# Seven products of halves in place of the down projection of both MLPs, in an fp32 two-layer streaming trunk

## The chip, the cores and the metric

The kernel runs on one core of one Trainium2 chip. The metric is the device time of one execution in microseconds; a timed comparison takes the median of several executions. The core has five engines that work through queues of their own: TensorE (PE, with its weight loads listed apart as PEld), VectorE (DVE), ScalarE (ACT), GpSimd (POOL) and SyncE (SP), which issues loads. Each engine takes its queue in order, and waits on semaphores that other engines and DMAs raise.

## The reference

One inference step over 1152 tokens (1024 of a new stream, 8 x 16 of running streams) through two layers of width 1024. What matters here is the MLP at the end of each layer and the next norm:

```python
def sq_relu_mlp(h, w_up, w_down):                 # w_up (1024, 4096), w_down (4096, 1024)
    return jnp.square(jax.nn.relu(h @ w_up)) @ w_down

xp = xp + op                                      # mixer's output
xp = xp + sq_relu_mlp(rmsnorm(xp, norm_ffn[layer]), w_up[layer], w_down[layer])
y_prompt = rmsnorm(xp, norm_final)                # after both layers
```

All data is fp32. The kernel keeps fp32 accuracy by splitting each operand into a rounded part and a remainder (`hi`, `lo`, type fp32r) and adding three matmuls for each product: hi*hi, hi*lo, lo*hi (`SPLIT`).

## The kernel before, in words

Activations lie with features on partitions and tokens along a row. `mixer0` and `mixer1` are the attention and convolution stages of the two layers. `rest(layer, ...)` does what follows each mixer: the output projection, then the up projection, then the down projection. The MLP's inner layer has 32 blocks of 128 rows (`NF`).

**Up projection.** `unit(m)`, m = 0 to 15, makes two of these blocks, 2m and 2m+1. It already works by seven products of halves: the input's feature halves and token halves (`combo`), and the weights' halves with their sums, made by `seven`. A product k is `mms(k, n, ...)`: 4 chunks of 128 features x 3 parts = 12 matmuls of 288 columns for each n (0 and 1, a quarter of the tokens each), so 24 for a product and 168 for a unit. `take(k, n)` adds the results from PSUM on DVE (L1400 to L1412). `done` multiplies a quarter by the norm's factor (DVE, L1386), applies relu and square (ACT, L1387 and L1388), and stores a token half of a block from the POOL queue (L1390) to a buffer in HBM, `hid_d`. The hidden rows lie in four tiles (`hids`: `th` and three called `hdm`), two for even units and two for odd ones.

**Down projection.** It loads the hidden blocks back whole (`down_h`, L1469, 128 x 1152), splits them, loads the weights in pieces of 128 x 512 (`down_w` through `staging`, L187), splits them, and takes four inner blocks at a time (`NB`): for each of 8 output chunks c and 3 token groups g of 384 (`G`), `down(j, c, g)` issues 4 x 3 = 12 matmuls of 384 columns (L1485) into a PSUM bank, and DVE adds the bank to the residual `x[c]` in SBUF (L1489). That is 8 x 8 x 3 x 12 = 2304 matmuls for a layer. On the last four blocks the code also prepares the next stage: norm statistics and split inputs for layer 1's mixer (`Then0`), or the final norm, transposes and stores (`Then1`).

`split(hi, lo, src)` is a copy on ACT (L180) and a subtraction on DVE (L181). PSUM has 8 banks, handed out in a ring by `bank`; a bank is taken again once its last reader is through. Tiles of a pool with one name are handed on in the same way.

**What sets the order.** The program is written out as a list of operations; a scheduler then sets the order on each engine by its own estimate of when operands and tiles come free. So weight loads and splits are moved up as soon as their tile is free, and stand in an engine's queue ahead of work that was written before them.

## Time and profile before

| | us |
|---|---|
| three timed runs | 2881.17, 2886.65, 2888.04 (median 2886.65) |
| profiled execution: its time / its span | 2879.29 / 2877.5 |
| PE busy in the span | 2778.7 (97%) |
| DVE / ACT / POOL busy | 2015.6 / 1264.4 / 282.3 |
| up projection, layer 0 / layer 1 | 644.6 to 1009.2 / 2093.7 to 2460.0 |
| down projection, layer 0 / layer 1 | 1009.2 to 1413.6 / 2460.0 to 2865.4 |

Times inside the span count from its start. Where two durations overlap (a matmul starts before the one ahead of it has drained), rates are read from start to start over many instructions, not from the mean duration. "Idle before" is the time an engine sat still ahead of a group, with what ended it. KB are 1024 bytes.

### The profile page before, as it was taken

The page shows a single profiled execution, that of the slowest core. Times are in us where ns is not written, and L with a number is a line of the kernel's source. Part 1 is how long each engine was busy: PE and PEld are TensorE (multiplying, and loading weights), DVE is VectorE, ACT ScalarE, POOL GpSimd, SP SyncE. Part 2 cuts the span into 40 slices and gives each one's busy share as a digit, 9 for nine tenths or more (in the row PEclk, how much of TensorE's full clock was granted, in tenths as well). Part 3 has the DMA queues.
Part 4 walks back from the last instruction along what each step waited for, and adds up shares of the span by engine and source line. Part 5 has one row for each costly group of instructions (what it writes and reads, how often), then busy time and mean ns, then how long its engine had stood idle before and what let it go on. Part 6 is the DMA issues. An engine that isn't in the chain of part 4 may idle for free.

```text
span 2877.5 us, 48092 instructions
## 1 busy us (share of the span) xinstructions
PE 2778.7 (97%) x18586; PEld 2674.3 (93%) x18586; DVE 2015.6 (70%) x3939; ACT 1264.4 (44%) x2644; POOL 282.3 (10%) x511
## 2 busy tenths in 40 slices
PE   8988988899999999999999999998999999999998
PEld 8987876799999999999999999997999999999998
DVE  8999999988666654444567777778786666644445
ACT  5344446665555531211355555556555554411112
POOL 1000101031000000000111111110310110000001
PEclk9999998999999999999999999999999999999999
DMA  4434346443332362321344444446532322732311
GB/s 152 131 102 127 114 123 205 147 162 117 106 105 94 131 232 77 109 79 46 107 141 133 135 143 139 134 132 220 180 123 94 102 99 102 251 102 67 110 34 66
DMA packets 136004, 357.70 MB, mean 124 GB/s; under 512 B 21232, under 2 KB 44976, under 8 KB 133728
## 3 DMA queue, kind: packets, MB, share of 16 engines
q1 hardware_dynamic: 105936, 252.06, 27.5%
q0 software_dynamic: 29696, 102.56, 10.5%
q8 instruction: 146, 2.39, 0.3%
q14 instruction: 82, 0.67, 0.1%
q10 hardware_dynamic: 144, 0.02, 0.0%
HBM read 252.90 MB, written 89.03 MB: 119 GB/s over the span
## 4 chain that ended last, share of the span: by engine, by line
PE 75%; DVE 16%; ACT 4%; issue 3%; DMA 2%; POOL 0%; DVEq 0%; SPq 0%; ACTq 0%; POOLq 0%
PE pd L1485 28%; PE um L1380 23%; PE psc L220 10%; DVE y L671 4%; DVE kp L847 2%; PE avc L404 2%; PE psoa L220 2%; PE tpc L392 2%; PE f L220 1%; DVE sg L849 1%; PE zc L1137 1%; DVE wla L181 1%; PE zc L1138 1%; PE psp L220 1%; PE zs L505 1%
## 5 line engine op out<-in xcount | busy, mean ns | idle before, releaser
L1489 DVE TENSOR_TENSOR sl<-sl,pd 128x384 f32<-128x384 f32 x384 | 211.6, 552 | 342.4 <-PE pd L1485 342.0
L220 PE MATMUL psc<-h,hl_wc 128*128 128x384 f32 x1728 | 328.2, 340 | 0.0
L220 PEld LDWEIGHTS psc<-h,hl_wc 128*128 128x128 f32 x1728 | 298.5, 189 | 13.4 <-issue 11.5
L1380 PE MATMUL um<-sl,hl_m 128*128 128x288 f32 x1548 | 240.3, 296 | 0.0
L1380 PEld LDWEIGHTS um<-sl,hl_m 128*128 128x128 f32 x1548 | 217.7, 188 | 0.0
L671 DVE SCALAR_TENSOR_TENSOR y<-u,dw,y 128x1024 f32<-128x1024 f32 (+1 forms) x232 | 176.4, 807 | 0.4
L220 PE MATMUL psp<-h,hl_wi 128*128 128x384 f32 x864 | 169.7, 345 | 0.2 <-ACT kps L896 0.2
L220 PEld LDWEIGHTS psp<-h,hl_wi 128*128 128x128 f32 x864 | 150.4, 191 | 6.4 <-issue 4.9
L1485 PE MATMUL pd<-hsm,wdm 128*128 128x384 f32 x864 | 150.8, 334 | 0.0
L1485 PEld LDWEIGHTS pd<-hsm,wdm 128*128 128x128 f32 x864 | 149.9, 188 | 0.0
L181 DVE TENSOR_TENSOR hl_m<-xr,hl_m 128x512 fp32r<-128x512 f32 x132 | 92.4, 700 | 57.1 <-ACT hl_m L180 55.8
L180 ACT ACTIVATE hl_m<-xr 128x512 fp32r<-128x512 f32 x132 | 82.2, 623 | 104.7 <-PE um L1380 83.2
L1387 ACT ACTIVATE hdm<-hdm 128x288 f32<-128x288 f32 x192 | 84.8, 442 | 91.7 <-DVE hdm L1386 90.9
L1380 PE MATMUL um<-sl,hl 128*128 128x288 f32 x756 | 119.4, 296 | 0.0
L1104 ACT ACTIVATE s<-s,mxc 128x640 f32<-128x640 f32 (+4 forms) x128 | 88.8, 694 | 59.8 <-DVE mxc L1101 58.1
L1380 PEld LDWEIGHTS um<-sl,hl 128*128 128x128 f32 x756 | 106.6, 188 | 0.8
L180 ACT ACTIVATE wdm<-st_wd 128x512 fp32r<-128x512 f32 x40 | 23.8, 624 | 171.2 <-PE pd L1485 144.8
L1101 DVE CUSTOM_DVE_ANT_0 s<-zc,bp 128x384 f32<-128x384 f32 (+3 forms) x128 | 66.0, 517 | 38.9 <-PE zc L1138 38.1
L180 ACT ACTIVATE whc<-tpc 128x512 fp32r<-128x512 f32 (+1 forms) x144 | 72.5, 523 | 47.0 <-PE tpc L392 46.1
L181 DVE TENSOR_TENSOR wlc<-tpc,whc 128x512 fp32r<-128x512 f32 (+1 forms) x144 | 83.5, 595 | 12.8 <-ACT whc L180 10.4
L1390 POOL DMA_DIRECT2D hid_d<-hdm x96 | 51.9, 540 | 412.9 <-ACT hdm L1388 334.7
L180 ACT ACTIVATE hl<-st_wd 128x512 fp32r<-128x512 f32 x20 | 12.6, 629 | 171.0 <-PE pd L1485 155.3
(495 smaller groups left out, 6997.6 us busy)
## 6 DMA issues: line engine op xcount, KB each, us to landing
hrm<-hid_d SPq DMA_DIRECT2D x64, 576.0 KB, 5.0
xr<-in_w_up_dram SPq DMA_DIRECT2D x64, 512.0 KB, 3.7
st_wd<-in_w_down_dram SPq DMA_DIRECT2D x128, 256.0 KB, 3.3
hid_d<-hdm POOLq DMA_DIRECT2D x96, 288.0 KB, 2.4
st_wc<-in_w_in_c_dram SPq DMA_DIRECT2D x48, 256.0 KB, 2.7
xm_d<-xo POOLq DMA_DIRECT2D x16, 576.0 KB, 3.5
xr<-xm_d SPq DMA_DIRECT2D x16, 576.0 KB, 4.6
xr_d<-xr POOLq DMA_DIRECT2D x16, 576.0 KB, 3.3
```

The source lines that it names most:

```text
L180: ACT(hi, src, AF.Copy)
L181: return tt(lo, src, f(hi), ALU.subtract)
L220: mm(ps()[:, :G], hl[:, a, at:at + P], act[g][k // 4][b][:, k % 4, :], start=n == 0, stop=n == len(todo) - 1)
L392: nc.tensor.transpose(tp[:, c0 + q * P:c0 + (q + 1) * P], blocks.get(j, tile_q), ident)
L404: mm(st["av"][:, o0:o0 + n], vs[:, j, i].rearrange("p a d -> p (a d)"), src[:, c0:c0 + n], start=st["done"] == 0, stop=st["done"] == nmm - 1)
L671: stt(src if j == CW - 1 else dst, src, wj, dst, ALU.mult, ALU.add)
L1101: nc.vector.tensor_tensor_reduce(s[:, c:c + m], z, b, -1.0, mx, ALU.add, ALU.min, new)
L1104: ACT(s[:, :n], s[:, :n], AF.Exp, bias=mx, scale=-1.0, accum_out=tot)
L1380: mm(banks[b, n][:, :TQ], w[:, a, c * P:c * P + P], combo(key, c)[:, h, n * TQ:n * TQ + TQ], start=k < 3 and c == 0 and i == 0, stop=c == ...
L1387: ACT(y, y, AF.Relu)
L1485: mm(ps[:, :G], w[:, a, c % 4 * P:c % 4 * P + P], hid[NB * j + e][b][:, g * G:g * G + G], start=n == 0, stop=n == 3 * NB - 1)
L1489: tt(xs, xs, ps[:, :G], ALU.add)
```

## The change

The down projection becomes seven products too. The 32 inner blocks are paired (2j, 2j+1, j = 0 to 15), the outputs are halved (512 features each) and the tokens are halved (576 each, `TW`). With a11, a12, a21, a22 for the weights of a pair (first index: output half, second: inner block) and b11, b12, b21, b22 for the hidden rows (first: inner block, second: token half), the hidden operands are b11 (product 0), t2 = b11 - t3 (1), b12 - b11 (2), b21 (3), t3 = b12 - b22 (4), b22 (5) and t4 = b21 - t2 (6). A product runs over all 16 pairs before the next one starts, in PSUM, so that an output tile is added to the residual only where a product ends.

- The up projection now stores the seven operands, 128 x 576 each, to `hb_d`. Four subtractions on DVE are added to a unit: t3, t2 and b12 - b11 in `done` (after.py's L1400 to L1402), and t4 in `last_sum` (L1365), which is called in the next unit, before its product 2.
- The down projection is a list of 112 items (`todos`): 7 products x 16 pairs. An item loads its hidden operand (L1506), splits it (128 x 576) and the weight (128 x 512), and issues 4 output chunks x 2 token quarters x 3 = 24 matmuls of 288 columns (L1577). The products run in four chains that each hold all 8 PSUM banks: (3), (0, 1, 4), (2, 5), (6). Loads are written four items ahead, splits two.
- Weights a11, a21 and a22 are loaded once and stay in SBUF (`resident`, L1493), in tiles that the up projection leaves. Sums of weights are made on DVE (L1527 to L1533). a12 and, for the last product, a22 are loaded by item.
- What follows each layer now starts from finished quarters of the result (`then0`, `then1`). At the start of layer 1's mixer the token groups are taken in the order 2, 0, 1. In layer 1 the last product is done for one token quarter and then the other; the transposed part of the output shrinks from 384 to 288 tokens.
- The statistics tiles change with it: one tile `t1` (128 x 1152) is a buffer for squares, and holds t3 and t2 during the up projection.

The diff, cut to its core:

```diff
-    hid_d = [dram.tile([NF, P, T], F32, name=f"hid_d{l}") for l in range(2)]
+    hb_d = [dram.tile([7, NF // 2, P, TW], F32, name=f"hb_d{l}") for l in range(2)]
...
-                if p == 0 and (n, g) in ((1, 0), (0, 1)):
-                    (nx.end if n else nx.run_rows)(NG - 1)
-                if g == 0:
+                if p == 0 and n < 2:
+                    if n == 0:
+                        nx.run_rows(g)
+                    elif g == 2:
+                        nx.end(0)
+                        nx.end(1)
...
-                    return (chunks_steps([0, 1], got, ahead, h, ks, lambda n, ps, g: staged(0, n, ps, g), "c")
+                    return (chunks_steps([0, 1], got, ahead, h, ks, lambda n, ps, g: staged(0, n, ps, g), "c", gs=(2, 0, 1))
...
+        extra = own("t1", F32)
...
+        t3, t2 = extra[:, :TW], extra[:, TW:]
+        def last_sum(m):
+            t4 = hids[m % 2 * 2 + 1][:, :TW]
+            tt(t4, t4, t2, ALU.subtract)
+            put(hb_d[layer][6, m], t4)
...
-                    put(hid_d[layer][2 * m + e, :, half * TW:half * TW + TW], hd[e][:, half * TW:half * TW + TW])
+                    b11, b12, b22 = hd[0][:, :TW], hd[0][:, TW:], hd[1][:, TW:]
+                    if (e, half) == (0, 1):
+                        tt(t3, b12, b22, ALU.subtract)
+                        tt(t2, b11, t3, ALU.subtract)
+                        tt(b12, b12, b11, ALU.subtract)
+                        for k, t in ((4, t3), (1, t2), (2, b12)):
+                            put(hb_d[layer][k, m], t)
+                    else:
+                        put(hb_d[layer][{(0, 0): 0, (1, 1): 5, (1, 0): 3}[e, half], m],
+                            hd[e][:, half * TW:half * TW + TW])
...
             for k in range(start, 7):
                 seven(7 * m + k + 2)
+                if m and k == 2:
+                    last_sum(m - 1)
+                if m == NF // 2 - 1 and k > 4:
+                    begin(k - 5)
...
+        chains = ((3,), (0, 1, 4), (2, 5), (6,))
+        out = {3: [(0, 0)], 0: [(0, 0)], 1: [(0, 1)], 4: [(1, 0), (1, 1)], 2: [(1, 1)], 5: [(0, 1)], 6: [(1, 0)]}
+        final = {0: (0, 0), 2: (1, 1), 5: (0, 1), 6: (1, 0)}
+        todos = [(k, (0, 1), j) for chain in chains for k in chain for j in range(NF // 2)]
+        if layer == 1:
+            todos[6 * 16:] = [(6, (n,), j) for n in range(2) for j in range(NF // 2)]
+        wd = ins["w_down"][layer]
...
+        def resident(kind, j):
+            to = {"a11": a11, "a21": a21, "a22": a22}[kind]
+            if j % 2 == 0:
+                if kind == "a22":
+                    tag = ("sl8", "sl9", "sl10", "sl11", "lo0", "lo1", "lo2", "xr3")[j // 2]
+                    t = own(tag, F32)
+                else:
+                    t = place(j // 2, 0 if kind == "a11" else 1, F32, f"w{name}")
+                to[j], to[j + 1] = halves_of(t)
+            row = 2 * j + (kind == "a22")
+            dma(to[j], wd[row][:, :512] if kind == "a11" else wd[row][:, 512:])
+        def load(i):
+            if i >= len(todos):
                 return
+            k, ns, j = todos[i]
+            if i == 0:
+                for n in range(2):
+                    t = own(f"xr{n}", F32)
+                    braw.extend([t[:, :TW], t[:, TW:]])
+            cols = slice(ns[0] * TQ, ns[-1] * TQ + TQ)
+            bs[i] = braw[i % 4][:, :cols.stop - cols.start]
+            dma(bs[i], hb_d[layer][k, j][:, cols])
+            if k in (3, 5) or k == 6 and ns[0] == 0:
+                streams[i] = staging(wd[2 * j + 1][:, 512:] if k == 6 else wd[2 * j + 1][:, :512], f"wd{layer}{i}")
...
+        def split_w(i):
...
+            if k == 3 or k == 6:
+                src = streams.pop(i)
+            elif k == 5:
+                src = streams.pop(i)
+                tt(src, src, a22[j], ALU.subtract)
+            elif k == 1:
+                tt(a21[j], a21[j], a11[j], ALU.subtract)
+                tt(a22[j], a22[j], a21[j], ALU.add)
+                src = a22[j]
+            elif k == 2:
+                tt(a11[j], a11[j], a22[j], ALU.add)
+                src = a11[j]
+            else:
+                src = a11[j] if k == 0 else a21[j]
+            if k == 6 and layer == 1:
+                w = pair(place(j // 2, j % 2, F32R, f"wk{name}"))
+            elif k == 6:
+                if j < 8:
+                    tag = ("sl8", "sl9", "sl10", "sl11", "lo0", "lo1", "lo2", "xr3")[j]
+                    asplit.append(pair(own(tag, F32R)))
+                w = asplit[j % 8]
+            elif i % 6 < 4:
+                w = sp.tile([P, 2, 512], F32R, "hl", f"hl_wd{layer}{i}")
+            else:
+                w = pair(few[i % 6 - 4])
+            split(w[:, 0], w[:, 1], src)
+            ws[i] = w
+        def begin(n):
+            if n == 0:
+                for i in range(4):
+                    load(i)
+            else:
+                prep(0)
+                prep(1)
...
+        def item(i):
+            k, ns, j = todos[i]
+            first = any(k == chain[0] for chain in chains) and j == 0
+            b, w = bs.pop(i), ws[i]
+            for m in range(4):
+                for n in ns:
+                    if first:
+                        banks[m, n] = bank(f"pd{layer}{k}{m}{n}")
+                    ps = banks[m, n][:, :TQ]
+                    for s, (a, h) in enumerate(SPLIT):
+                        mm(ps, w[:, a, m * P:m * P + P], b[:, h, (n - ns[0]) * TQ:(n - ns[0]) * TQ + TQ],
+                           start=first and s == 0, stop=j == NF // 2 - 1 and s == 2,
+                           skip_group_check=not any(k == chain[0] for chain in chains))
+                    if j == NF // 2 - 1:
+                        for e, half in out[k]:
+                            xs = x[4 * e + m][:, half * TW + n * TQ:half * TW + n * TQ + TQ]
+                            tt(xs, xs, ps, ALU.add)
+            if j == NF // 2 - 1 and k in final:
+                later.extend(then(x, *final[k], None if len(ns) > 1 else ns[0], sq))
...
+        sq = Turns([extra[:, :TW], extra[:, TW:]])
+        for i in range(len(todos)):
+            if i == 3:
+                last_sum(NF // 2 - 1)
+            if 2 <= i < 18:
+                resident("a11", i - 2)
+            if 14 <= i < 30:
+                resident("a21", i - 14)
+            if 16 <= i < 32:
+                resident("a22", i - 16)
+            c = {n: m for m, n in enumerate((6, 7, 8, 9, 40, 41, 42, 43))}.get(i)
+            if c is not None:
+                x[c] = own(f"sl{c}", F32)
+                dma(x[c], xr_d[layer][c])
+            load(i + 4)
+            prep(i + 2)
+            item(i)
+            if i == 104 and soon:
+                soon()
+            for _ in range(1 + (len(later) > len(todos) - i)):
                 if later:
                     later.pop(0)()
...
+        def then0(x, e, half, n, sq):
+            n1.sq = sq
+            cols = slice(half * TW, half * TW + TW)
+            cs = range(4 * e, 4 * e + 4)
+            def square(c):
+                n1.square(x[c][:, cols], c, cols, c == (4 if half else 0))
+                put(x_d[:, c, cols], x[c][:, cols])
+            squares = [lambda c=c: square(c) for c in cs]
+            splits = [lambda c=c: n1.split(x[c][:, cols], c, cols) for c in cs]
+            if (e, half) == (0, 0):
+                early.extend(splits)
+                return squares
+            if (e, half) == (1, 1):
+                return squares + splits + early
+            if (e, half) == (0, 1):
+                return squares + splits
+            return [lambda: n1.end(2)] + [go for two in zip(splits, squares) for go in two]
```

How this moves instructions, at three places. First, DVE in an up projection's unit, around the additions of its last product (k = 6). `um` is a PSUM bank, `tm` a partial result, `rm` the norm's factor, `hl` split weights, `xr` raw weights; PE, ACT and DVE in brackets are waits on these engines, DMASW on a POOL store. Before:

```order
L181 TENSOR_TENSOR hl_m_7846<-xr_6076,hl_m_7846 128x512 [waits Activation_49]
L1412 TENSOR_TENSOR hdm_61_6750<-um_7577,tm_6082 128x288 [waits DMASW0_49,PE_49]
L1386 TENSOR_TENSOR hdm_61_6750<-hdm_61_6750,rm_6842 128x288 [waits DVE_49]
L1412 TENSOR_TENSOR hdm_61_6750<-um_7591,tm_6083 128x288 [waits PE_49]
L1386 TENSOR_TENSOR hdm_61_6750<-hdm_61_6750,rm_6842 128x288 [waits DVE_49]
L181 TENSOR_TENSOR hl_m_7877<-xr_6075,hl_m_7877 128x512 [waits Activation_49]
```

and now:

```order
L181 TENSOR_TENSOR hl_m_8095<-xr_6078,hl_m_8095 128x512 [waits Activation_49]
L1429 TENSOR_TENSOR hdm_51_6724<-um_7819,tm_6082 128x288 [waits DMASW5_49,PE_49]
L1400 TENSOR_TENSOR t_6087<-th_6723,hdm_51_6724 128x576 [waits DMASW0_49,Activation_49]
L1394 TENSOR_TENSOR hdm_51_6724<-hdm_51_6724,rm_6818 128x288 [waits DVE_49]
L1401 TENSOR_TENSOR t_6087<-th_6723,t_6087 128x576 [waits DMASW1_49,DVE_49]
L1402 TENSOR_TENSOR th_6723<-th_6723 128x576
L1429 TENSOR_TENSOR hdm_51_6724<-um_7833,tm_6082 128x288 [waits PE_49]
L181 TENSOR_TENSOR hl_6079<-xr_6077,hl_6079 128x512 [waits Activation_49]
L1394 TENSOR_TENSOR hdm_51_6724<-hdm_51_6724,rm_6818 128x288 [waits DVE_49]
```

Three subtractions of 576 columns stand between the two quarters of the last product; the first of them waits for ACT's square and for the store that last read its tile.

Second, DVE in layer 0's down projection. Before, some way into it (`pd` is a PSUM bank, `lo`, `hl`, `xr` and `sl` split operands or the residual, `hrm` hidden rows loaded back; DMAHW is a load from SP's queue):

```order
L1489 TENSOR_TENSOR sl_10695<-sl_10695,pd_10839 128x384 [waits PE_49]
L181 TENSOR_TENSOR xr_10959<-hrm_50_10956,xr_10958 128x1152 [waits DMAHW0_49,Activation_49]
L181 TENSOR_TENSOR lo_6085<-st_wd_10952,lo_6085 128x512 [waits DMAHW1_49,Activation_49]
L1489 TENSOR_TENSOR sl_10697<-sl_10697,pd_10861 128x384 [waits PE_49]
L181 TENSOR_TENSOR lo_6086<-st_wd_11004,lo_6086 128x512 [waits DMAHW2_49,Activation_49]
L181 TENSOR_TENSOR xr_11057<-hrm_51_11054,xr_11056 128x1152 [waits DMAHW3_49,Activation_49]
L1489 TENSOR_TENSOR sl_10697<-sl_10697,pd_10875 128x384 [waits PE_49]
```

and now, in the first product, around the split of item 8's hidden operand (the fourth row, `th`); `wm` and the `sl` in L1530 are resident weights, `tm`, `th` and the `xr` in L181 hidden operands:

```order
L1529 TENSOR_TENSOR wm_11_11311<-wm_11_11311,wm_10_10900 128x512 [waits DMAHW5_49]
L181 TENSOR_TENSOR hl_6079<-st_wd_10972,hl_6079 128x512 [waits DMAHW1_49,PE_49,Activation_49]
L181 TENSOR_TENSOR th_10714<-xr_10662,th_10714 128x576 [waits DMAHW4_49,Activation_49]
L1530 TENSOR_TENSOR sl_11313<-sl_11313,wm_01_11239 128x512 [waits DMAHW0_49,DVE_49]
L181 TENSOR_TENSOR hl_6080<-st_wd_11007,hl_6080 128x512 [waits DMAHW3_49,PE_49,Activation_49]
L181 TENSOR_TENSOR xr_10720<-xr_10662,xr_10720 128x576 [waits DMAHW7_49,Activation_49]
L1529 TENSOR_TENSOR wm_11_11311<-wm_11_11311,wm_10_10900 128x512 [waits DMAHW4_49]
L1530 TENSOR_TENSOR sl_11313<-sl_11313,wm_01_11239 128x512 [waits DMAHW5_49]
L181 TENSOR_TENSOR tm_10762<-xr_10663,tm_10762 128x576 [waits DMAHW2_49,Activation_49]
```

The additions from PSUM are gone from here; the sums of weights for product 1 (L1529, L1530), written for items 32 to 47, have moved up into the first product and wait there for their loads, with the splits queued behind them. With two sums for product 2 (L1533), 28 sums of weights stand ahead of the first product's eight additions to the residual.

Third, SP's queue at the same place, which before held only `hrm` and `st_wd` in turn:

```order
L187 DMA st_wd_11007<-in_w_down_dram 128x512 [waits DMAHW5_49,DVE_49]
L1493 DMA wm_60_11237<-in_w_down_dram 128x512 [waits DMAHW4_49]
L1493 DMA wm_11_11311<-in_w_down_dram 128x512
L1506 DMA xr_10663<-hb_d_116 128x576 [waits DMAHW6_49,DMASW3_49,DVE_49]
L187 DMA st_wd_11043<-in_w_down_dram 128x512 [waits DMAHW7_49,DMAHW0_49,DVE_49]
L1493 DMA sl_11313<-in_w_down_dram 128x512
L1493 DMA wm_70_11309<-in_w_down_dram 128x512 [waits DMAHW1_49]
L187 DMA st_wd_11077<-in_w_down_dram 128x512 [waits DMAHW2_49,DVE_49]
L1506 DMA xr_10662<-hb_d_116 128x576 [waits DMAHW3_49,DVE_49]
```

Two resident pieces now stand between the loads of one item and those of the next. From the load of item 6's operand to that of the last resident piece whose sum stands ahead of the first additions, the queue holds 15 hidden operands, 10 streamed weights and 27 resident pieces.

More of the change, by code (lines that the diff above doesn't have):

```diff
@@ L1263, in old @@
                 dma(x[order[n]], xm_d[layer][:, order[n], :])
-        nx = Next(2 * layer + 1, rst, mp, name)
+        nx = Next(2 * layer + 1, rst, Turns([extra[:, g * G:g * G + G] for g in range(NG)]), name)
         todo = []
@@ L1464, in down_h @@
-        def down_h(n):
-            if n in hid or n >= NF:
-                return
-            src = place(4 + n % 4 // 2, n % 2, F32, f"hr{name}{n}")
-            dma(src, hid_d[layer][n])
-            j, e = divmod(n, NB)
-            if n < NB:
-                sets[0, e] = [place(e, i, F32R, f"hs{name}") for i in range(2)]
-            elif n < 2 * NB:
-                sets[1, e] = ([slots[8 + 2 * e + i] for i in range(2)] if e < 2 else
-                              [own(f"xr{2 * e - 4 + i}", F32R) for i in range(2)])
-            hid[n] = sets[j % 2, e]
-            split(*hid[n], src)
@@ new lines, in split_b @@
+        def split_b(i):
+            while len(bsplit) < 4 and len(bsplit) <= i:
+                bsplit.append(pair(own(("th", "xr2", "tm0", "tm1")[len(bsplit)], F32R), T))
+            n = bs[i].shape[1]
+            t = bsplit[i % 4][:, :, :n]
+            split(t[:, 0], t[:, 1], bs[i])
+            bs[i] = t
+        def split_w(i):
+            k, ns, j = todos[i]
+            if ns == (1,):
+                ws[i] = ws[i - 16]
+                return
+            if k == 3 or k == 6:
[25 more added lines that the diff above has]
+            ws[i] = w
@@ L1529, in tile_trunk, with __init__, acc, split @@
     class Next:
-        def __init__(self, which, rst, pl, name):
-            self.which, self.pl, self.name, self.rst = which, pl, name, rst
-            self.h = [[None, None] for _ in range(NG)]
-            self.acc, self.r, self.diag, self.rows = [None] * NG, {}, {}, {}
-            self.all = None
-        def split(self, xs, c, g):
-            if self.h[g][c // 4] is None:
-                self.h[g][c // 4] = new_h(g, c // 4, self.name)
-            hi, lo = (t[:, c % 4, :] for t in self.h[g][c // 4])
+        def __init__(self, which, rst, sq, name, accs=None):
+            self.which, self.sq, self.name, self.rst, self.accs = which, sq, name, rst, accs
+            self.h = new_hs(name)
+            self.r, self.diag, self.rows = {}, {}, {}
+            self.sums = self.all = None
+        def acc(self, at, n):
+            if self.accs:
+                return self.accs[at // G]
+            if self.sums is None:
+                self.sums = self.rst.tile([P, T], F32, "acc", f"acc{self.name}")
+            return self.sums[:, at:at + n]
+        def split(self, xs, c, cols):
+            tiles = chunks.setdefault(self.name, {})
+            for i in range(2):
+                if (c, i) not in tiles:
+                    tiles[c, i] = place(c, i, F32R, self.name)
+            hi, lo = (tiles[c, i][:, cols] for i in range(2))
             nw = norms[:, self.which, c:c + 1]
```

245 lines of the change are left out of this document (100 added, 145 removed).

## The prediction

> **What bounds the kernel now.** I read the page first, then busy times by stage, then the chain of waits, then the groups of DVE, then loads. The page's engine line and slices (40 of 71.9 us):
>
> ```profile
> PE 2778.7 (97%) x18586; PEld 2674.3 (93%) x18586; DVE 2015.6 (70%) x3939; ACT 1264.4 (44%) x2644; POOL 282.3 (10%) x511
> PE   8988988899999999999999999998999999999998
> DVE  8999999988666654444567777778786666644445
> ```
>
> PE is full everywhere; DVE has six to eight tenths in the up projections (slices 9 to 13, 29 to 33) and four to five in the down projections (14 to 19, 34 to 39). By stage (busy us and instructions of each engine; last granted clock, DMA share, GB/s): 15 units of layer 0's up projection, then the two down projections, then the tail:
>
> ```profile
> core 0: us, PE busy (x) PEld busy (x) DVE busy (x) ACT busy (x) POOL busy (x), PEclk, DMA share, GB/s
> 667.00:1001.20 334.20, 334.20 (x2519) 334.20 (x2518) 225.31 (x436) 174.66 (x379) 32.43 (x60) 1.00 0.31 104
> 1009.20:1413.60 404.40, 403.71 (x2316) 402.98 (x2315) 204.35 (x341) 94.79 (x148) 13.52 (x25) 1.00 0.31 105
> 2460.00:2865.40 405.40, 404.88 (x2322) 403.86 (x2321) 198.45 (x333) 84.85 (x130) 7.01 (x14) 1.00 0.28 94
> 2865.40:2877.50 12.10, 3.75 (x32) 3.22 (x29) 6.11 (x15) 3.57 (x7) 2.68 (x5) 0.82 0.64 236
> ```
>
> PE is busy 403.71 of 404.40 us at clock 1.00: these stages are as long as their matmuls. The chain of waits (start, length) agrees, running through PE alone:
>
> ```profile
> 666.97 329.71 PE um L1380 x2483
> 1011.37 382.27 PE pd L1485 x2189
> 2117.71 336.10 PE um L1380 x2531
> 2461.96 373.95 PE pd L1485 x2141
> ```
>
> A matmul of 288 columns takes 329.71/2483 = 132.8 ns (layer 1: 336.10/2531, the same; 334.20/2519 = 132.7), one of 384 columns 382.27/2189 = 174.6 (373.95/2141 = 174.7). Both streams change weights at every matmul, so weight loads are in these rates.
>
> **The matmuls.** A down projection has 2304 matmuls of 384 columns; it gets 112 x 24 = 2688 of 288 (in layer 1 the last product's are regrouped, with the same number and size). That is the stream of an up projection: 16 x 168 = 2688, also 288 columns, also three parts. So 2688 x 0.1327 = 356.7 us in place of 404.4 and 405.4: 96.4 us off both. Statistics matmuls and transposes, some 2 us a layer (1 to 3), lie in the old stages and only move: +4. Net -92.4.
>
> **DVE in the up projection.** Each unit gets four subtractions of 128 x 576. DVE's rows in the 15 units, and the 1152-column split of the whole run:
>
> ```profile
> L181 DVE TENSOR_TENSOR hl_m<-xr,hl_m 128x512 fp32r<-128x512 f32 x61 | 42.0, 688 | 28.3 <-ACT hl_m L180 27.5
> L1386 DVE TENSOR_TENSOR hdm<-hdm,rm 128x288 f32<-128x288 f32 x74 | 33.8, 457 | 2.4
> L1412 DVE TENSOR_TENSOR hdm<-um,tm 128x288 f32<-128x288 f32 x30 | 13.7, 455 | 8.4 <-PE um L1380 8.4
> L1345 DVE TENSOR_TENSOR xr<-xr 128x512 f32<-128x512 f32 x15 | 10.4, 691 | 0.5
> L181 DVE TENSOR_TENSOR hsm<-hrm,hsm 128x1152 fp32r<-128x1152 f32 x32 | 43.3, 1353 | 7.1 <-ACT hsm L180 7.1
> ```
>
> Between 688 ns at 512 columns and 1353 at 1152, 576 columns cost 688 + 64 x 665/640 = 755 ns; four are 3.0 us a unit. A unit is 334.2/15 = 22.3 us, with DVE busy 15.0 and idle 7.3. Whom DVE waits for there, and ACT (total us, times, longest):
>
> ```profile
> DVE hl_m L181 <- ACT hl_m L180: 30.9, 28, 2.6
> DVE tm L1400 <- PE um L1380: 18.7, 19, 1.2
> DVE hdm L1406 <- PE um L1380: 11.5, 24, 0.7
> ACT hl_m L180 <- PE um L1380: 42.4, 23, 2.7
> ACT hl L180 <- PE um L1380: 25.6, 15, 2.6
> ```
>
> DVE's idle time goes back to PE: directly, or through ACT, which waits for PE to free a weight tile. That is slack, which a later DVE uses up without holding PE. ACT's square, and a store (issue, then KB and us to its landing):
>
> ```profile
> L1388 ACT ACTIVATE hdm<-hdm 128x288 f32<-128x288 f32 x192 | 85.1, 443 | 5.5
> L1390 POOL DMA_DIRECT2D hid_d<-hdm x96 | 51.9, 540 | 412.9 <-ACT hdm L1388 334.7 <-ACT tm L1398 72.4 <-ACT hl L180 3.1
> hid_d<-hdm POOLq DMA_DIRECT2D x96, 288.0 KB, 2.4
> ```
>
> New waits: t3 for ACT's relu and square, mostly over by then, since the first quarter of product 6 ends a half product (1.6 us) later; t4 for the store of its operand, about a multiplication, two ACT passes, the issue and the landing, 0.5 + 0.9 + 0.5 + 2.4 = 4.3 us behind the last addition, against 6.4 us until DVE reaches it behind product 1's additions. With 1 us for both DVE needs 19 of 22.3 us. Behind t4 stand the split of a weight used later and product 2's additions, which PE needs read only when product 5 takes up their banks, two products (6.4 us) after product 2's end. So 0; if slack and waits don't give, this is the second rival. POOL issues 7 stores a unit for 4: 7 x 0.54 = 3.8 of 22.3 us, hidden.
>
> **The first product, where DVE and the loads are dense.** An item lasts 24 x 0.1327 = 3.19 us on PE. Its splits are one of 576 and one of 512 columns: 0.755 + 0.69 = 1.45 us of DVE, and on ACT, by
>
> ```profile
> L180 ACT ACTIVATE hl_m<-xr 128x512 fp32r<-128x512 f32 x132 | 82.2, 623 | 104.7 <-PE um L1380 83.2
> ```
>
> 2 x 0.62 and a little more, 1.3 us; both hidden. But 28 sums of weights have moved ahead of the first eight additions to the residual. Up to there DVE owes, from these sums on, 28 x 0.69 + 13 x 0.755 + 14 x 0.69 + 0.755 = 39.6 us; it begins some 7 us into the stage, after the last unit's rest, and PE wants the banks at 16 x 3.19 = 51: 44 us. The queue's 15 hidden operands (288 KB) and 37 weight pieces (256 KB) are 14.1 MB, to land in much the same 44 us: 320 GB/s. What loads reach when they are dense (GB/s; KB and median landing time, first 1025 to 1050 us, then 995 to 1010):
>
> ```profile
> 1010.00:1020.00 10.00, 9.31 (x53) 8.84 (x53) 5.24 (x10) 3.00 (x7) 1.08 (x2) 1.00 1.03 415
> DMA packets 2543, 6.81 MB, mean 272 GB/s; under 512 B 288, under 2 KB 288, under 8 KB 2541
> st_wd<-in_w_down_dram SPq DMA_DIRECT2D x10, 256.0 KB, 4.0
> st_wd<-in_w_down_dram SPq DMA_DIRECT2D x3, 256.0 KB, 11.8
> ```
>
> At 415 GB/s 14.1 MB take 34 us and nothing is late; at 272 they take 52, 8 us late. Whatever is late holds item 16, whose banks wait for additions queued behind the sums. I take the middle, 4 us a layer, since neither margin (39.6 or 41 of 44 us) has room for many waits: +8 (0 to 16). The Trainium skill, "DMA: Bandwidth & Descriptors", section "Where 436 GB/s comes from", says that about 358 GB/s of HBM bandwidth per core binds loads; by it 14.1 MB take 39 us, nothing is late, and this term would be 0. The trace's 415 GB/s lies above that limit, so here it isn't one.
>
> **Additions at the ends of products.** Before, DVE adds every bank:
>
> ```profile
> L1489 DVE TENSOR_TENSOR sl<-sl,pd 128x384 f32<-128x384 f32 x384 | 211.6, 552 | 342.4 <-PE pd L1485 342.0
> ```
>
> 211.6 us of DVE go; 64 additions of 288 columns a layer (0.456 each) come. None of it was on the path, since PE is full. At a product's end the eight banks take 3.6 us, PE's next item 3.2, and a bank is wanted again an item later: covered. Product 4 adds each bank twice: 16 x 0.456 = 7.3 us; the eighth bank is free 7.9 us after its last item began, and PE wants it at 3.19 + 7 x 0.40 = 6.0. At most 1.9 us; starts 0.38 apart would leave 0.7. I take 1 a layer: +2.
>
> **Into layer 1's mixer, and the tail.** Now PE waits for the last group's statistics:
>
> ```profile
> 1417.94 1.65 PE L280 MATMUL rr_h<-sq_h,ones 128*128 128x384 f32 x2 [3.70 <-DVE sq_h L276]
> 1418.82 10.51 PE L220 MATMUL psc<-h,hl_wc 128*128 128x384 f32 x48
> 2867.54 0.55 DVE L294 TENSOR_TENSOR sq_fin<-sq_fin,sq_fin 128x384 f32<-128x384 f32 x1
> L1544 DVE SCALAR_TENSOR_TENSOR h<-sl,norms,h 128x384 fp32r<-128x384 f32 x24 | 14.8, 617 | 13.3 <-ACT h L1543 13.3
> ```
>
> After the change token group 2 comes first: its 48 matmuls (8.4 us at 174.6 ns) need only finished halves. Meanwhile DVE has 1 us of additions left, four splits (0.62 us at 384 columns by the last row, so about 0.8), four additions of squares (0.755) and the statistics (some 1.5): 8.7 us, while the last split is wanted after 8.4 + 7/8 x 4.2 = 12. Of 3.7 us I take 3 back (0 to 3.7). In the tail four chunks end together where one did; the last square's addition came at 2867.54, 2.1 us behind PE, and comes up to a few tenths later: +0.5 (0 to 2).
>
> **Sum:** -92.4 + 0 + 8 + 2 - 3 + 0.5 = -84.9. The profiled execution, 2879.3 us (span 2877.5 and 1.8 around it), becomes 2794; it lies 7.4 under the median 2886.65, so I expect a median of 2802. The terms' own ends give -97 to -69: 2790 to 2818.
>
> **Rivals.**
> *The first product starves (2830).* Loads of an item are released by splits a few items ahead, four to eight DVE rows (2.8 to 5.5 us) before the sum that waits for them. At a landing of 4.0 us that nearly fits; at the 11.8 of the fullest stretch, or a bit above 5, each of about five successive rounds loses 2 to 6 us, and the lag adds up: some 18 us a layer in place of 4, +28. For it: in 1010 to 1020 the DMA share is 1.03 already. Against: that stretch is 20 us long and PE lost 0.7 us in it.
>
> *The up projection is bound by DVE, and the change is slower (2930).* If DVE's 7.3 us of idle time stay in series with its work, a unit becomes 15.0 + 7.3 + 3.0 + 1 = 26.3 us, 4.0 more; 32 units lose 128 us: 2930. It decides once a unit grows by 84.9/32 = 2.7 us. For it: the longest DVE wait is for ACT, and t3 adds another. Against: ACT's own waits for PE, above.
>
> *Matmuls don't get cheaper with fewer columns (slower, 2910).* If a matmul had a fixed cost as large as the streaming of 288 columns, 5376 would cost what 4608 did. The rows give (174.6 - 132.7)/96 = 0.44 ns a column and some 7 ns fixed. The Trainium skill, "TensorE: Matmul & The Clock Gate", section "Back-to-back issue gap", gives measured spacings of about 81 ns at 128 columns and 131 at 512 in streams that load weights. By its line (102 and 114 ns at 288 and 384) the change would cost some 21 us, and end near 2910; both rates of this trace lie far off it, so it gets 2%.
>
> **Chances and range.** Forecast 66%; starving, 20%; DVE-bound, 6%; fixed cost, 2%; 6% for something unnamed, either way (3% of it at no change). 0.3% (about 9 us) is what a measurement can tell: faster 0.90, within 0.3% 0.03, slower 0.07. The range 2789 to 2834 takes in the forecast's ends and the starving case.
>
> **What would show it.** Right: down stages of 360 to 368 us with PE full at about 133 ns a matmul; units still 22.3 us, DVE busy 18; a gap on PE at item 16, some 51 us into each stage, that ends on L1583 behind L1529 and L1530, and one of about 1 us at item 64; no wait of 3.7 us at the mixer's start. Starving: DVE idle on loads (st_wd, wm, xr) in the first 50 us, and PE idle there. DVE-bound: units of 24 us or more, with um waiting for DVE. The forecast falls if 288-column matmuls in eight open banks run slower than 140 ns, or if PE loses over 20 us a layer.

## The result: faster, by a third of what was forecast

The changed kernel takes 2857.06 us (median of four runs, 2855.06 to 2857.8) against 2883.91 us for the kernel before on the same chip (2878.12 to 2888.04). The ratio is 0.9907, with a 95% interval of 0.9887 to 0.9928: 27 us off, where 85 were forecast. The predicted time of 2802 us and its range up to 2834 us were missed.

The page of the changed kernel begins with less work for PE and more for DVE, as it should:

```profile
span 2854.7 us, 50855 instructions
PE 2708.8 (95%) x19362; PEld 2594.2 (91%) x19362; DVE 2141.5 (75%) x4201; ACT 1376.3 (48%) x2898; POOL 330.5 (12%) x599
```

PE's share of the span fell from 97 to 95%: it now waits somewhere. The stages, read from the first and the last matmul of each (us):

| stage | before | changed | difference | forecast |
|---|---|---|---|---|
| up projection, layer 0 | 364.6 | 387.4 | +22.8 | 0 |
| down projection, layer 0 | 404.4 | 370.1 | -34.3 | about -41 |
| mixer of layer 1 | 680.1 | 677.5 | -2.6 | -3 |
| up projection, layer 1 | 366.3 | 385.3 | +19.0 | 0 |
| down projection, layer 1 | 405.5 | 378.0 | -27.5 | about -41 |
| tail | 11.9 | 12.0 | +0.1 | +0.5 |

(The forecast for the down projections is half of -92.4 + 8 + 2 each.) Two thirds of the missing time, 41.8 us, went in the up projections, which were costed at nothing; the other third, some 20 us, in the down projections.

The stretches of layer 0, with the same columns as before (the up projection; the first product of the down projection up to PE's return; the rest of the down projection):

```profile
644.40:1031.80 387.40, 370.66 (x2713) 365.37 (x2712) 281.68 (x561) 184.95 (x416) 62.43 (x112) 0.99 0.41 142
1031.80:1094.58 62.78, 53.12 (x386) 51.15 (x385) 44.73 (x72) 24.30 (x43) 2.70 (x5) 0.97 0.92 316
1094.58:1401.73 307.15, 307.15 (x2305) 307.15 (x2305) 189.13 (x310) 130.02 (x213) 7.60 (x14) 0.99 0.49 150
```

PE is idle 17 us in the up projection and 10 in the first product, and full in the rest. In the up projection it is also busy 8 us longer than before (370.7 us for 362.3), part of it at a lower clock behind some of the gaps (last section). In the rest: 307.15/2305 = 133.3 ns a matmul, so the product itself costs what was forecast.

What releases PE, in the waits of the whole run:

```profile
PE um L1388 <- DVE hdm L1423: 25.1, 17, 2.3
PE pd L1577 <- DVE sl L1583: 13.9, 3, 6.1
PE pd L1577 <- DVE tm L181: 5.0, 7, 1.2
```

L1423 adds product 4 of an up projection's unit; its bank is the one that PE needs for product 6. The chain of waits, which ran through PE alone before, now goes through a store of nearly each unit:

```profile
752.79 6.71 DMA hb_d<-hdm
778.84 5.51 DMA hb_d<-hdm
791.87 8.22 PE um L1388 x60
802.50 4.53 DMA hb_d<-hdm
...
1094.58 307.31 PE pd L1577 x2304
```

The operation that waits for it is t4 (L1365). DVE's waits in 13 units of layer 0, 699.29 to 1009.46 us (all there are):

```profile
DVE hdm L1365 <- DMA hb_d<-hdm: 46.7, 13, 5.9
DVE hl_m L181 <- ACT hl_m L180: 30.4, 35, 1.8
DVE hl L181 <- ACT hl L180: 12.8, 14, 1.1
```

That is 3.6 us a unit for the store and 3.3 for ACT. No wait for PE is left, where two of the three rows of DVE quoted before were such: DVE is late all the time, and PE follows it. What ACT's copies for these splits wait for has changed too. In 13 units before (696.95 to 986.93 us), and then in the same 13 units of the changed kernel:

```profile
ACT hl_m L180 <- PE um L1380: 36.8, 20, 2.7
ACT hl L180 <- PE um L1380: 25.6, 15, 2.6
ACT hl_m L180 <- DVE xr L1338: 9.0, 2, 5.4
```

```profile
ACT hl_m L180 <- DVE xr L1338: 45.8, 6, 8.6
ACT hl L180 <- DVE xr L1338: 28.2, 5, 6.3
ACT hl_m L180 <- PE um L1388: 12.8, 3, 6.1
```

Before, the copies waited for PE (62.4 us); now they wait for a sum of DVE itself (L1338, 74.0 us), which stands behind t4 in DVE's queue. So DVE waits for ACT, which waits for DVE.

One wait for the store, on DVE, from the last addition of a unit (L1429) on, with POOL's issue of the store and SP's load of the next raw weights in the same 6 us:

```profile
775.79 0.45 DVE L1429 TENSOR_TENSOR hdm<-um,tm 128x288 f32<-128x288 f32 x1
...
778.84 0.54 POOL L1406 DMA_DIRECT2D hb_d<-hdm  x1 [1.89 <-ACT tm L1415]
778.85 0.81 DVE L1417 TENSOR_TENSOR tm<-um,tm 128x288 f32<-128x288 f32 x2
778.96 0.33 SPq L1323 DMA_DIRECT2D xr<-in_w_up_dram  x1
784.37 0.76 DVE L1365 TENSOR_TENSOR hdm<-hdm,t 128x576 f32<-128x576 f32 x1 [4.71 <-DMA hb_d<-hdm]
```

The store lands 5.5 us after its issue, not 2.4, and product 1's additions (L1417), which were to keep DVE busy until then, are through at once, because PE is ahead.

### The profile page after: what moved, and what is told of

Its sections match the earlier page's. It is cut to its first block, busy times and chain, and to the rows that moved or that the text cites. A ratio compares the mean times of both kernels' runs of the same rounds, so it can differ in the third digit from the quotient of the medians.

```text
span 2854.7 us, 50855 instructions
## 1 busy us (share of the span) xinstructions
PE 2708.8 (95%) x19362; PEld 2594.2 (91%) x19362; DVE 2141.5 (75%) x4201; ACT 1376.3 (48%) x2898; POOL 330.5 (12%) x599
## 4 chain that ended last, share of the span: by engine, by line
PE 51%; DVE 24%; DMA 9%; issue 8%; ACT 7%; POOL 0%; SPq 0%; DVEq 0%; POOLq 0%; ACTq 0%
PE pd L1577 21%; PE psc L220 10%; PE um L1388 6%; DMA hb_d<-hdm 4%; DVE y L669 4%; DVE kp L843 2%; PE avc L401 2%; PE tpc L389 2%; DVE sg L845 1%; PE f L220 1%; PE psoa L220 1%; DVE hdm L1394 1%; DVE hl_m L181 1%; DMA st_wd<-in_w_down_dram 1%; DVE wla L181 1%
## 5 line engine op out<-in xcount | busy, mean ns | idle before, releaser
L1577 PE MATMUL pd<-tm,hl_wd 128*128 128x288 f32 x1536 | 210.4, 295 | 4.9 <-DVE tm L181 3.9
L1577 PEld LDWEIGHTS pd<-tm,hl_wd 128*128 128x128 f32 x1536 | 205.2, 189 | 6.8 <-DVE tm L181 5.0
L181 DVE TENSOR_TENSOR tm<-xr,tm 128x576 fp32r<-128x576 f32 (+1 forms) x120 | 85.3, 714 | 70.0 <-ACT tm L180 70.0
L180 ACT ACTIVATE tm<-xr 128x576 fp32r<-128x576 f32 (+1 forms) x120 | 77.6, 647 | 119.2 <-PE pd L1577 98.2
L181 DVE TENSOR_TENSOR hl_m<-xr,hl_m 128x512 fp32r<-128x512 f32 x132 | 92.3, 700 | 44.7 <-ACT hl_m L180 44.7
L1577 PE MATMUL pd<-th,hl_wd 128*128 128x288 f32 x768 | 107.8, 295 | 2.3 <-DVE hdm L1429 2.2
L1577 PE MATMUL pd<-tm,hl 128*128 128x288 f32 x768 | 105.9, 295 | 1.2 <-DVE tm L181 1.2
L1577 PE MATMUL pd<-xr,hl_wd 128*128 128x288 f32 x768 | 106.9, 295 | 0.0
L1577 PEld LDWEIGHTS pd<-th,hl_wd 128*128 128x128 f32 x768 | 103.5, 189 | 3.2 <-DVE hdm L1429 2.7
L1577 PEld LDWEIGHTS pd<-tm,hl 128*128 128x128 f32 x768 | 103.3, 188 | 2.1 <-DVE tm L181 2.1
```

The source lines that it names most:

```text
L180: ACT(hi, src, AF.Copy)
L181: return tt(lo, src, f(hi), ALU.subtract)
L1577: mm(ps, w[:, a, m * P:m * P + P], b[:, h, (n - ns[0]) * TQ:(n - ns[0]) * TQ + TQ], start=first and s == 0, stop=j == NF // 2 - 1 and s == ...
```

## The experiments

There are two questions. Why does a unit take 23.9 us in place of 22.3? And why do 12 us a layer go in the down projection, where the gap at item 16 is 6.1? Times of a whole run are medians, those of a stage and all rows are from the profiled execution; ratios are to runs of the kernel before on the same chip.

### 1. t4 written over t2

```diff
-            tt(t4, t4, t2, ALU.subtract)
-            put(hb_d[layer][6, m], t4)
+            tt(t2, t4, t2, ALU.subtract)
+            put(hb_d[layer][6, m], t2)
```

> Edit: t4 is written over t2 (and stored from there) in place of over its operand b21, so that it no longer waits for the store of b21; the work of DVE, POOL and the queues is the same. Theory W (the wait on that store makes DVE late): DVE's 3.4 us a unit at L1365 go, 18 us of work and 3.2 us of waits for ACT fit in 22.3 us, and the up projections fall from 387.4 and 385.3 us to 365 to 368; the time falls from 2857 by 36 to 42, to 2815 to 2821. Rival N (the four subtractions themselves are too much work): the up projections stay above 380 us and the time above 2847.

Measured: 2838.63 us (ratio 0.9851, 0.9833 to 0.9868). Up projections 377.8 and 376.0 us: 9 to 10 us came back in each, half of what theory W wanted, and rival N's bound is not met either. DVE's waits in 13 units of layer 0 show where the rest went:

```profile
DVE s1m L1336 <- DMA xr<-in_w_up_dram: 32.6, 12, 3.4
DVE hl_m L181 <- ACT hl_m L180: 16.4, 25, 1.1
DVE hl L181 <- ACT hl L180: 12.4, 13, 1.1
DVE t L1365 <- DMA hb_d<-t: 8.8, 4, 3.0
```

The store's wait has shrunk, and a new one of 2.5 us a unit stands at L1336, the first sum of the next unit's raw weights, whose load has not landed. That operation stood behind t4 in the queue, and the wait for the store had covered it.

### 2. The sums of weights behind the first product's additions

```diff
+        def behind(ins):            # an order on DVE, not a wait
+            tc.add_manual_dep(ins.ins, marks[3].ins.name, ...)
...
-                tt(a21[j], a21[j], a11[j], ALU.subtract)
+                behind(tt(a21[j], a21[j], a11[j], ALU.subtract))
...
-                            tt(xs, xs, ps, ALU.add)
+                            marks[k] = tt(xs, xs, ps, ALU.add)
```

> Edit: the first sum of weights for product 1 (and so all that need it) is kept behind the last addition of the first product on DVE; loads and everything else as in the change. Theory G (the additions are late because they stand behind the sums): the two gaps of 6.1 us at item 16 go, and with them the slow matmuls after them (1.7 and 2.8 us): about -16 us, to 2841 (2838 to 2846). Rival L (loads are what is late, and hold the splits of items 12 to 16 just the same): gaps of 3 us or more stay, time above 2850.

Measured: 2829.79 us (0.9821, 0.9804 to 0.9839). Down projections of 357.8 and 365.0 us for 370.1 and 378.0: 12.3 and 13.0 us came back, more than theory G's 8 or 9 a layer. Rival L fell. The same stretch (the last column is GB/s, loads and stores together), and what moved from 1050 to 1090 us:

```profile
1029.20:1091.90 62.70, 61.84 (x466) 61.61 (x466) 40.13 (x67) 27.64 (x49) 2.69 (x5) 1.00 1.02 378
DMA packets 7862, 15.52 MB, mean 388 GB/s; under 512 B 872, under 2 KB 872, under 8 KB 7857
q1 hardware_dynamic: 7857, 15.46, 104.2%
```

PE is full, and the DMAs move 378 GB/s where the change had 316; in the 40 us of the second row, where nearly all is loads (`q1`), it is 388. So the loads of the change were not at their limit. The edit asks for nothing but another order on DVE, so it is DVE's order that had held them up; that a DVE which stands at one load frees no tile for the next is the likely way, and no run shows it by itself.

### 3. Both edits

> Both edits together. If the two losses are separate: 2857 - 40 - 16 = 2801 (2797 to 2808). If a faster up projection only delivers DVE and the queues earlier into the same crowded first product, some of the gain is lost there: 2810 or more, with gaps on PE in items 1 to 16.

Measured: 2813.06 us (0.9759, 0.974 to 0.9777). Up projections 378.9 and 377.9, down 358.4 and 364.0: each edit gives the same as alone, and the first product loses nothing more. The time alone would fit the second alternative (2810 or more); the down projections rule it out. The expected sum was missed because edit 1 gave 18 us and not 40.

### 4. Edit 1 with 3 us more work for DVE

```diff
-                        tt(t3, b12, b22, ALU.subtract)
+                        for _ in range(5):
+                            tt(t3, b12, b22, ALU.subtract)
```

> t4 over t2, and in each unit the subtraction for t3 four more times (the same result again): 4 x 0.755 = 3.0 us more work for DVE, no new wait. If DVE's waits for ACT are in series with its work: a unit is 18 + 3.2 + 3.0 = 24.2 us, 1.9 over PE's 22.3, and 31 units lose 59 us against t4 over t2 alone: about 2876. If those waits are slack that a later DVE uses up, as the prediction took them: 18 + 3.0 + 1 = 22 us, under 22.3, and the time is that of t4 over t2 alone within 10 us: about 2818.

Measured: 2879.0 us (0.9988, 0.9979 to 0.9997), 40 us above edit 1; up projections 398.8 and 394.7. So the unit of edit 1 has little slack: most of the work comes on top of the waits, as the first alternative has it. Of the 59 us expected only 40 came. DVE's busy time grew by 2.5 us a unit and not 3.0, since rows that follow one another directly overlap (see the last section), and the waits for ACT shrank by 1.1 us (table below), so that a unit grew by 1.45 us. That the time came near the 2876 us expected is luck: it was reckoned from 2817 us for edit 1, which took 2839.

### 5. A third edit: L1336 behind product 4's additions

```diff
-                tt(s1, a21, a22, ALU.add)
+                go = tt(s1, a21, a22, ALU.add)
+                if m > 1:
+                    tc.add_manual_dep(go.ins, parts[1].ins.name, ...)   # order on DVE
...
-                    tt(to(1, 1, n), ps, tmp["u3", n], ALU.add)
+                    parts[1] = tt(to(1, 1, n), ps, tmp["u3", n], ALU.add)
```

> The two edits together and a third: the sum of raw weights at L1336 is kept behind the additions of product 4 in its unit; with both edits DVE stood 2.6 us a unit at it, waiting for the load of these weights, which starts as the five stores do. Theory C (a chain of stalls, one behind the other: with the store's wait gone the next operation in DVE's queue waits for a load): the up projections fall from 378.9 and 377.9 us to 365 to 369, the time from 2813 by 19 to 26, to 2787 to 2794. Rival N (DVE's work and its waits for ACT fill the unit anyway): up projections above 374 us, time above 2805.

Measured: 2787.03 us (0.9671, 0.9655 to 0.9688), as theory C has it. It is the fastest version: 93 us (3.3%) below the 2880.22 us of the kernel before on the same chip, and some 70 below the change. Up projections 364.6 and 367.7, down 356.6 and 361.7. All of DVE's waits in 13 units, 698.03 to 988.02 us:

```profile
DVE hdm L1426 <- PE um L1391: 23.1, 26, 1.1
DVE tm L1422 <- PE um L1391: 17.8, 26, 1.1
DVE th L1397 <- PE um L1391: 15.8, 14, 1.1
DVE hdm L1397 <- PE um L1391: 13.7, 12, 1.1
```

DVE has the same work and waits for PE alone. Not only the wait for the load is gone: those for ACT, 2.8 us a unit in experiment 3, are gone too. The sums at L1336 to L1338 feed ACT's copies, which feed DVE's splits. In experiment 3 these copies waited 41.1 us in 13 units for the sum of L1338; here they wait 3.9 us for the same sum (L1341 in this kernel), and DVE finds them done.

### 6. All three edits with 3 us more work for DVE

> All three edits, and the subtraction for t3 four more times a unit (3.0 us more of DVE's work, no new wait). With no wait for a DMA left, this measures the slack itself. If waits for ACT (30 us in 14 units, 2.1 a unit) stay in series: 18 + 2.1 + 3.0 = 23.1 us for a unit, 0.8 over 22.3, so 31 units lose 25 us against the three edits alone. If only the work counts: 21.0 us, under 22.3, and no more than 5 us are lost.

Measured: 2793.51 us (0.969, 0.9675 to 0.9706), 6.5 us above experiment 5 with intervals that overlap; the up projections of the profiled execution are 365.0 and 365.6 us, no longer than without. The same work that cost 40 us in experiment 4 costs next to nothing here. The waits for ACT that the expectation of a loss assumed were not there any more. The 14.9 units of 667 to 1000 us, PE and DVE:

```profile
667.00:1000.00 333.00, 333.00 (x2510) 333.00 (x2509) 283.37 (x548) 170.05 (x373) 56.15 (x104) 1.00 0.42 148
```

DVE is busy 85% of the time and PE never waits.

### 7. No subtractions, seven stores

```diff
-                        tt(t3, b12, b22, ALU.subtract)
-                        tt(t2, b11, t3, ALU.subtract)
-                        tt(b12, b12, b11, ALU.subtract)
-                        for k, t in ((4, t3), (1, t2), (2, b12)):
+                        for k, t in ((4, b12), (1, b11), (2, b12)):
...
-            tt(t4, t4, t2, ALU.subtract)
```

> As the change with sums behind (2829.8 us), but the four subtractions of a unit are left out: seven tiles are stored all the same, raw operands in place of t2, t3, t4 and the difference, so this leaves out part of the computation. It keeps the seven stores and takes away DVE's work and the wait for the store. Theory W/C (DVE's work with its waits in series binds the unit): up projections from 385.9 and 384.0 to 365 to 368, time 2790 to 2796. Rival Q (seven stores on one queue and their bytes slow the unit): up projections stay above 375 us, time above 2808.

Measured: 2793.27 us (0.9694, 0.9679 to 0.9708); up projections 367.5 and 365.6, as theory W/C has it. Seven stores on one queue cost nothing, and rival Q fell. DVE's waits in 13 units (700.17 to 990.16 us) are of both kinds here:

```profile
DVE hl_m L181 <- ACT hl_m L180: 30.6, 33, 2.6
DVE tm L1413 <- PE um L1387: 16.6, 17, 1.2
DVE hl L181 <- ACT hl L180: 12.2, 10, 2.2
```

The waits for ACT are 3.3 us a unit although DVE is not late. They are not of the change's kind, though: ACT's copies in their turn wait for PE, as before the change (64.5 us in these two rows), and hardly for DVE's sum at L1338 (8.2 us):

```profile
ACT hl_m L180 <- PE um L1387: 36.1, 15, 2.7
ACT hl L180 <- PE um L1387: 28.4, 17, 2.6
```

### 8. The third edit alone

> The change with the third edit alone: only the sum at L1336 is kept behind product 4's additions; t4 still overwrites its operand and the sums of weights stay ahead in the first product. Theory C (stalls one behind the other): DVE does not wait at L1336 in the change, and its 3.4 us a unit for the store at L1365 stay, so up projections stay above 380 us and the time at 2851 to 2863. Rival O (where L1336 stands is what matters, and it made DVE late from the start): up projections fall to about 366, time about 2816.

Measured: 2814.17 us (0.9756, 0.9732 to 0.9781); up projections 368.0 and 365.8. Theory C fell, and rival O was right: theory C said that nothing would change while t4 waits for its store. That wait is still there, and PE is full. From the waits of 13 units (703.94 to 993.93 us):

```profile
DVE hdm L1368 <- DMA hb_d<-hdm: 34.2, 13, 3.2
DVE hdm L1426 <- PE um L1391: 23.1, 26, 1.1
...
DVE hl_m L181 <- ACT hl_m L180: 1.9, 9, 0.2
```

t4 (L1368 here) waits 2.6 us a unit, ACT is waited for 0.15 us, and the rest of the time goes to waits for PE. ACT's copies wait 6.9 us in all for DVE's sums, where they waited 74.0 in the change. In this order the unit can carry the store's wait. Why the order ends the waits between ACT and DVE is read from these rows; no run takes it apart further.

### 9. t4 over t2 and the third edit, without the second

> t4 over t2 and L1336 behind product 4, with the sums of weights still ahead of the first product's additions. If the losses are separate: up projections of 365 to 368 as with all three edits (2787), and the down projections' 12 us each stay, 2787 + 25 = 2812 (2807 to 2818). If the first product only starved because DVE came late out of the up projection: its gaps shrink too, and the time is below 2800.

Measured: 2813.26 us (0.9763, 0.9744 to 0.9782); up projections 366.4 and 368.8, down 369.7 and 372.3. The losses are separate, as the first alternative has it: a first product that is handed over in time loses almost as much (layer 0: 369.7 for 370.1; in layer 1, 372.3 for 378.0, some of it came back). And experiments 8 and 9 are the same: once L1336 stands behind product 4's additions, where t4 is written makes no difference.

### What the runs add up to in the up projection

DVE's time per unit in layer 0, from 13 units each (busy time and waits by what released them, divided by 13; what is left to the sum are gaps too short for a row). The stretch of the change, whose DVE is 216.67/13 = 16.67 us busy a unit, and that of experiment 5:

```profile
699.29:1009.46 310.17, 295.67 (x2187) 292.09 (x2185) 216.67 (x424) 141.29 (x321) 49.11 (x91) 0.99 0.38 134
```

```profile
698.03:988.02 289.99, 289.99 (x2187) 289.99 (x2186) 217.76 (x430) 145.81 (x325) 49.09 (x91) 1.00 0.41 143
```


| kernel | unit | work | for PE | for ACT | for DMA |
|---|---|---|---|---|---|
| before | 22.31 | 14.93 | 3.75 | 2.82 | 0.35 |
| the change | 23.86 | 16.67 | 0 | 3.32 | 3.59 |
| 1, t4 over t2 | 23.22 | 16.84 | 0 | 2.85 | 3.18 |
| 4, the same, more work | 24.67 | 19.31 | 0 | 1.76 | 3.28 |
| 7, no subtractions | 22.31 | 14.92 | 2.83 | 3.29 | 0.80 |
| 8, third edit alone | 22.31 | 16.72 | 2.68 | 0.15 | 2.63 |
| 5, all three edits | 22.31 | 16.75 | 5.42 | 0 | 0 |
| 6, the same, more work | 22.31 | 19.15 | 2.89 | 0 | 0.17 |

In every row work and waits for ACT and DMA come to less than 22.3 us where PE is full, and to the whole unit, within 0.4 us, where it is not. No single wait is the cause. The change adds 1.7 us of work and 3.2 of waits for DMA to a DVE that had 3.75 us left; with the 0.5 more for ACT that is 1.7 too much, and a unit is 1.55 us longer. Taking away the waits for ACT (experiment 8) or the new work and the store's wait (experiment 7) is enough; taking away only the store's wait is not, because the load's wait behind it takes its place.

## Why the prediction was wrong, step by step

**The matmuls: right.** 112 x 24 matmuls of 288 columns at 132.7 ns were forecast to take 356.7 us a layer; in experiment 5 the down projections are 356.6 us, without a gap on PE, and 361.7, of which 1.6 are a gap where the last product begins and the rest was not looked into. The measured 133.3 ns leaves no room for the rival of a fixed cost per matmul.

**"DVE's idle time goes back to PE ... That is slack": this step failed, together with the next, and the two cost 42 us.** It took all 7.3 us of DVE's idle time in a unit for slack, on the ground that ACT in its turn waits for PE. In the kernel before, that was so for the copies that DVE's splits wait for: 62.4 us for PE in 13 units, against 11.4 for DVE's sums. In the changed kernel those waits for PE fell to 12.8 us, as a later engine uses them up; but the copies now waited 74.0 us for DVE's own sum, so that the 3.3 us a unit in which DVE waits for ACT came in series with its work. Only the 3.75 us in which DVE itself waited for PE were used up without loss. Experiment 8 shows that this is needed for the loss: with 0.15 us of waits for ACT left, the same work and 2.6 us of waiting for the store fit into 22.3 us.

**"With 1 us for both": this failed too.** t3 waits for nothing, as forecast. t4 waits 3.6 us a unit. The 4.3 us from the last addition to the landing became 8.1 (776.24 to 784.37 us in the rows above; the store lands 5.5 us after its issue, among three other stores and 1 MB of raw weights), and the 6.4 us until DVE would reach t4 became 3.4 (to 779.66), since product 1's results were there before DVE was. The forecast took both durations from a unit in which DVE is in time. The work, on the other hand, was 1.7 us and not 3.0. With both put right the sum would have read 14.9 + 1.7 + 2.8 + 3.6 = 23.0 us and more, over 22.3. By the same figures either error alone would not have shown: 14.9 + 1.7 + 2.8 + 1 = 20.4 us with the waits for ACT in series, 14.9 + 1.7 + 3.6 = 20.2 with the store's wait. That edit 1 gave only half back agrees: with the store's wait shrunk, the load's wait at L1336 took its place, and the sum stayed over 22.3.

**The rival of a DVE-bound up projection** named this mechanism, with 6%, at a price of 128 us. That was too high as this was too low: it put all idle time in series, the waits for PE too. The truth lies between, 42 us, and so the sign of the whole stayed that of the forecast. Its mark, PE's um waiting for DVE, is in the trace; "24 us or more" was just missed (23.9).

**The first product: the mechanism right, the size a third.** The gap on PE at item 16 is there in both layers, ending on L1583 behind L1530 and L1529. PE, then DVE just ahead of it, in layer 0:

```profile
1094.58 4.88 PE L1577 MATMUL pd<-th,hl 128*128 128x288 f32 x24 [6.13 <-DVE sl L1583]
...
1092.79 0.68 DVE L1529 TENSOR_TENSOR wm<-wm,wm 128x512 f32<-128x512 f32 x1
1093.39 0.68 DVE L1530 TENSOR_TENSOR lo<-lo,wm 128x512 f32<-128x512 f32 x1
1093.99 2.27 DVE L1583 TENSOR_TENSOR sl<-sl,pd 128x288 f32<-128x288 f32 x6
```

The term was 4 us a layer (0 to 8), and experiment 2 gives 12.3 and 13.0. The 6.1 us of the gap are inside those bounds; what the term left out are five or six smaller waits before it (3.5 us in layer 0, 4.8 in layer 1: the first at the handover from the up projection, the others for splits of hidden operands), and the slow matmuls after it (1.5 and 2.6 us). The rival of a starving first product (18 us a layer, 20%) lies nearer to that than the forecast's 4. Its mark is in the trace, DVE idle on loads (6.5 us at L1529 and 1.5 at L1530 in layer 0's first product); but it blamed the loads for what their place in DVE's queue did, as experiment 2 shows with the same loads. The 415 GB/s from which the forecast took its better bound counted stores too: of 4.15 MB in those 10 us 3.27 were loads, 327 GB/s. Experiment 2 shows that the loads do reach what was needed: 388 GB/s over 40 us. The Trainium skill, "DMA: Bandwidth & Descriptors", section "Where 436 GB/s comes from", sets about 358 GB/s for transfers between HBM and SBUF on one core; the 388 GB/s lie above it.

**The additions at the switch from product 4 to 2: not there.** +1 us a layer was taken; PE runs from item 16 to the end of layer 0's down projection in one piece (2304 matmuls in the chain above). In layer 1 a gap of 1.7 us, not foreseen, stands where the last product begins.

**Into layer 1's mixer: right.** -2.6 us against -3; the wait of 3.7 us is gone, one of 1.0 us is left. **The tail: right**, +0.1 against +0.5.

With the terms that failed put at nothing, the prediction's sum is -92.4 - 3 + 0.5 = -94.9 us. Experiment 5's ratio on the same base, 2886.65 x 0.9671, gives -95.0. That they agree to a tenth is luck: the two profiled executions differ by 91.0.

## What to carry to other kernels

Before work is added to an engine that seems to have time left, split its idle time by what ended it. What ends on the engine that sets the pace is slack. A wait for a third engine is slack only as long as that engine waits for the one that sets the pace: here ACT's copies did so before, and once DVE was late they waited for DVE, so that the wait came on top of the new work, as did the wait for the store of DVE's own result. An operation that stands early in an engine's queue and there waits for its data holds up all that stands behind it; ordering it behind work with a deadline gave 25 us in the two down projections (experiment 2) and 39 in the two up projections (experiment 8), with no work removed. And a wait that is taken away must be followed to the next operation in that queue before its length is counted as gain.

## What the runs showed of the hardware that was not expected

PE comes back slowly from a long gap. The 24 matmuls after the gap of 6.1 us took 4.88 us in layer 0 and 5.98 in layer 1, where 24 of them usually last 3.34; the granted clock is the third number from the end of each row (the ten microseconds after it are at full clock again):

```profile
1094.58:1099.46 4.88, 4.88 (x26) 4.88 (x27) 4.88 (x12) 0.09 (x1) 0.00 (x0) 0.67 0.92 313
1099.46:1110.00 10.54, 10.54 (x82) 10.54 (x81) 10.51 (x18) 4.49 (x8) 0.00 (x0) 1.00 0.98 358
2529.17:2535.15 5.98, 5.98 (x26) 5.98 (x27) 5.55 (x12) 0.11 (x1) 0.00 (x0) 0.52 0.98 359
```

So these two gaps cost 1.5 and 2.6 us, 25 and 43%, more than their length. The Trainium skill, "TensorE: Matmul & The Clock Gate", section "HAM oscillation — how this bites in real kernels", warns of idle gaps over about 3.4 us for this reason; the two gaps of 6.1 us agree with it. Shorter gaps cost nothing more or did so only at times. The 24 matmuls that begin 0.5 us after the end of a gap of 1.45 us (at 2469.09 us) took 3.33 us, the usual time. But of two gaps of 2.2 us in the up projection, both ended by L1423, the first was followed by half the clock, so that 3.4 us is no safe bound here, and the second by the full one; the rows are some 10 matmuls from the end of each gap:

```profile
767.00:769.53 2.53, 2.53 (x10) 2.53 (x11) 1.84 (x4) 1.99 (x5) 0.50 (x1) 0.50 0.30 117
910.73:912.10 1.37, 1.37 (x10) 1.37 (x11) 1.27 (x3) 0.87 (x3) 0.49 (x1) 1.00 0.25 98
```

What decides between the two was not looked into.

DVE's rows overlap where they follow one another without a wait: four subtractions of 0.755 us, which were costed at 3.0 us a unit, added 1.7 to its busy time. From a unit of the change:

```profile
799.46 0.75 DVE L1401 TENSOR_TENSOR t<-hdm,t 128x576 f32<-128x576 f32 x1
800.13 0.75 DVE L1402 TENSOR_TENSOR hdm<-hdm 128x576 f32<-128x576 f32 x1
```

The starts lie 0.67 us apart, 0.08 less than a row's length. Most rows of a packed DVE do so; a row that reads what the row just before it wrote does not (at 791.36 us L1423 of 0.45 us, and L1394, which reads its result, 0.49 later). So the work shrinks when it is packed: the lengths of DVE's rows add up to 18.4 us a unit in the change, in which it is busy 16.7 us, and to 15.7 and 14.9 in the kernel before.
